# S5 rotation tables from two short power ladders, squares of x summed on VectorE, and other ranks for the input and table tasks

## The chip, the core and the metric

The kernel runs on one NeuronCore of a Trainium2 chip. Its engines are TensorE (PE in the profile; its weight loads PEld), VectorE (DVE), ScalarE (ACT) and GpSimd (POOL), and SyncE (SP) issues most DMAs. The metric is the device time of one execution in microseconds (us), as the median of several. The profile comes from one execution with the hardware profiler.

## What is computed

One decoder layer on x of 1024 x 1024 float32. Three branches share one input projection, and their gated outputs go through one output projection; a gated per-layer input embedding and a final norm follow.

```python
hn = rms_norm(h, norm_g[i])
proj = hn @ w_in[i]
rg_x, rg_gate, gq, gk, gv, gz, gb, ga, s5_u, s5_gate = split_columns(proj)
...
y_rg = rg_lru(xr, ...) * silu(rg_gate)
y_gdn = gdn_branch(gq, gk, gv, gz, gb, ga, ...)          # 8 heads, gated delta rule in chunks
y_s5 = s5_ssm(s5_u, ...)                                  # 32 groups of 16 channels, 64 complex states each
    bu = einsum('gnc,sgc->sgn', b_bar, ub)
    _, xs = associative_scan(linear_combine, (lam_bar, bu))
    y = real(einsum('gcn,sgn->sgc', c_mat, xs)) + d_g * ub
z5 = gelu(y_s5); y_s5 = z5 * sigmoid(z5 @ s5_w_glu + s5_b_glu) * silu(s5_gate)
h = h + concatenate([y_rg, y_gdn, y_s5]) @ w_out[i]
gate = sigmoid(rms_norm(h, ple_norm_g[i]) @ ple_w_gate[i])
h = h + gate * (p[i] @ ple_w_proj[i])
return rms_norm(h, final_norm_g)
```

## The kernel before, in words

Products of float32 accuracy are made of three fast ones: each operand is split into a rounded high half and the rest (`hhi`, `hlo` for the normed input; `whi`, `wlo` for a weight), and hi·hi, lo·hi and hi·lo are summed in PSUM. A projection of one block of 128 columns is 48 such matmuls of 512 columns: two halves of the sequence, eight 128-row blocks k of the input, three products each (`project`). The weight's halves are made by one ScalarE cast (`whi`) and one VectorE subtraction (`wlo`) for each block.

The program begins with the product of p and its projection (`ple_proj`, tiles `ph`, `pl`, 96 matmuls). Beside it `norm_x` prepares the input: for each half of the sequence, squares of the eight blocks of x on ScalarE (`squares`), their column sums, a reciprocal square root in some 13 tiny VectorE steps, a broadcast through TensorE (`scale`), and for each block (`split`) one VectorE product into `xt`, one ScalarE cast into `hhi` and one VectorE subtraction into `hlo`.

Then the blocks are projected in a fixed order: x0 s0 e0 g0 x1 s1 e1 g1 x2 s2 e2 g2 x3 s3 e3 g3 (x and e: RG-LRU input and gate of a tile of 128 channels; s and g: S5 input and gate), k0 k1 k2 q0 v0 z0 (DeltaNet heads 0 to 2), and then k3 q1 v1 z1, k4 and so on, with the DeltaNet work of the heads between them. k4 is asked for only when the state chain of head 0 is done.

S5 is worked in tiles of eight groups. `s5_base` computes the powers of the states once; `s5_tables` makes for each tile the matrices `s_Q`, `s_G`, `s_Kp` and the rotations `s_C`, `s_S` (cosine and sine of 1 to 128 steps of eight positions, 64 states of eight groups in two partition halves). `s5_post` uses them: product of `s_QT` with the input `s_U`, rotation by `s_C` and `s_S` (one swap of partition halves by DMA, `s_Vs`), a scan (`s_Z`), rotation back (`s_Zs`, `s_X`), and the products `s_MT`·`s_U` + `s_G`·`s_X`. `s5_out` reads the result back in another layout (`s_Yc`), adds the direct term and applies gelu.

All of this is issued by a planner in the kernel's own code: work is a list of generator tasks, sorted by a rank from the table `PRIO` (lower first). After each projection matmul, `tick` issues the steps of those tasks that its price model calls ready, and each engine's instructions are then pinned in the order of issue. So the ranks decide at build time in which order VectorE, ScalarE and TensorE meet their work, and no engine overtakes at run time. `need` and `wait` hold back further projections until given tasks are issued.

Of the kernel before, what the change touches and what calls it, by code (L numbers as in the profile page):

```python
# [22 lines left out]
P = 128  # L23
# [12 lines left out]
ORDER = [(z[0], int(z[1])) for z in "x0 s0 e0 g0 x1 s1 e1 g1 x2 s2 e2 g2 x3 s3 e3 g3".split()]  # L36
SLOTS = dict(raw=2, cy=1, kT=4, dec=2, AT=3, qT=2, AQ=2, vn=2, sz=2, XT=2, kd=1, on=1, sA=1, sW=1)
# [8 lines left out]
class Trunk:  # L46
# [9 lines left out]
    PRIO = dict(squares=2, colsum=2, scale=2, split=2, drain=-1, save=-0.5, conv=1, gates=2, blocks=2, part_g=1, s5_out=1, shift=-1, k_post=1, q_post=1, v_post=-0.5, chain=1, chain_out=-1, finish=1, solve=1, levels=1, glu_prep=0.5, pre=1, glu_post=2, split_late=1, split_soon=-0.5, add=-0.5, ple_norm=2, s5_base=0.5, s5_tables=2, decay=2, decay_late=-1, wstream=-1, mstream=0.5)  # L56
# [283 lines left out]
    def norm_x(self, hpool, sp, startup, key):  # L340
# [23 lines left out]
        def squares(half, box, sums):  # L364
            box.append(self.ps(self.psg, [P, 4, KB]))
            for k in range(KB):
                yield "a", lambda: there[half, k] <= self.now
                z = sq[k % 2][:, k // 2 % 2]
# [8 lines left out]
        def scale(half, box, sums):  # L377
            yield "v", lambda: len(sums) == KB and all(t.done for t in sums)
            ss = sp.tile([P, 4], F32, name=f"xss{half}")
            nc.vector.tensor_reduce(out=ss, in_=box[0], axis=mybir.AxisListType.X, op=ALU.add)  # L380
            z = self.rstd_of(sp, ss, 1.0 / D, EPS, 4, f"xr{half}", 1)
            while True:
                try:
                    next(z)
                except StopIteration as e:
                    r = e.value
                    break
            yield "pe", self.psg
            rb = self.ps(self.psg, [P, 512], KB)
            for t in range(4):  # L390
                self.mm(out=rb[:, t * P:(t + 1) * P], lhsT=r[:, t:t + 1].to_broadcast([P, P]), rhs=self.ident, start=True, stop=True)
            for k in range(KB):
                self.spawn(split(half, k, rb), "v")
# [11 lines left out]
        for half in range(2):  # L405
            box, sums = [], []
            self.spawn(squares(half, box, sums), "a", room=lambda half=half: there[half, 0] <= self.now and self.room(self.psg))
            self.spawn(scale(half, box, sums), "v", room=lambda sums=sums: len(sums) == KB)
# [312 lines left out]
    def s5_base(self, keep, pool):  # L721
# [10 lines left out]
        wide = pool.tile([P, 32, 28], F32, name="s_w", bufs=1)  # L732
        yield "v"
# [64 lines left out]
        for j in range(8):  # L798
            l = 7 - j
            cpy(Aq[H0, :, j], pr[H0, :, l])  # L800
            cpy(Aq[H1, :, j], pi[H1, :, l])
            ng(Bq[H0, :, j], pi[H0, :, l])
            cpy(Bq[H1, :, j], pr[H1, :, l])
            if j % 2:
                yield
# [5 lines left out]
        c8, s8 = keep.tile(sh, F32, name="s_c8"), keep.tile(sh, F32, name="s_s8")  # L811
# [11 lines left out]
        ng(s8[H1], s8[H1])  # L823
        self.s5r = (c8, s8, R8)

    def s5_tables(self, i, pool, tabs):
# [52 lines left out]
        c8, s8, R8 = self.s5r  # L879
        v.tensor_copy(out=C[:, :, 0], in_=c8[:, gs])  # L880
        v.tensor_copy(out=Sn[:, :, 0], in_=s8[:, gs])
        n = 1
        uw = t.rearrange("p g l o -> p (g l o)")
        u, w = (uw[:, 512 * z:512 * z + 512].rearrange("p (g k) -> p g k", g=8) for z in range(2))
        while n < P:
            bc = lambda a: a[:, :, n - 1:n].to_broadcast([P, 8, n])
            self.cmul(v, C[:, :, n:2 * n], Sn[:, :, n:2 * n], C[:, :, :n], Sn[:, :, :n], bc(C), bc(Sn), u[:, :, :n], w[:, :, :n])
            n *= 2
            yield
        Kp = self.slot("AT", [16, 8, P], "s_Kp")  # L890
        for q in range(2):
            pool_ = (self.psc, self.pso)[q]
            yield "pe", lambda: part.done and part.ready <= self.now and self.room(pool_)
            pt = self.ps(pool_, [16, 4, P])
            for k in range(4):
                gg = 4 * q + k
                self.mm(out=pt[:, k, 0:16], lhsT=Qf[:, gg, 112:128], rhs=G0[:, gg, :], start=True, stop=True)
                self.mm(out=pt[:, k, 16:128], lhsT=Qf[:, gg, 112:128], rhs=Gf[:, gg, 0:112], start=True, stop=True)
            yield "a"
            nc.scalar.copy(out=Kp[:, 4 * q:4 * q + 4, :], in_=pt)  # L900
        tabs.extend((QT, Kp, Gf, C, Sn, R8[:, gs]))
# [27 lines left out]
    def s5_post(self, i, uP, tabs):  # L929
# [75 lines left out]
    def s5_out(self, i, uP, box):  # L1005
# [4 lines left out]
        yield "v"  # L1010
        nc.vector.scalar_tensor_tensor(out=f(Yc), in0=f(uP), scalar=self.s5d[:, i:i + 1], in1=f(Yc), op0=ALU.mult, op1=ALU.add)
# [614 lines left out]
    def build(self):  # L1626
        tc, nc = self.tc, self.nc
        with ExitStack() as st:
# [28 lines left out]
            with ExitStack() as s5s:  # L1657
# [9 lines left out]
                self.s5d = self.load(s5k, "s5_d", [P, 4])  # L1667
# [7 lines left out]
                for kind, i in ORDER:  # L1675
                    if kind == "s":
# [47 lines left out]
def layout(x, norm_g, w_in, rg_lambda, gdn_a_log, gdn_dt_bias, **kw):  # L1724
# [39 lines left out]
def program(shapes):  # L1764
    nc = bacc.Bacc("TRN2", target_bir_lowering=False, num_devices=1)
# [13 lines left out]
```

## Time and profile before

| | |
|---|---|
| median of 3 runs | 1248.16 us (1247.47 to 1253.04) |
| profiled execution: its time, its span | 1246.3 us, 1244.6 us |
| TensorE busy | 1134.6 us (91%), mean granted clock 0.956 |
| VectorE busy | 798.5 us (64%) |
| ScalarE busy | 552.4 us (44%) |
| GpSimd busy | 158.7 us (13%) |

Busy shares are means over stages with different limits. Times in the rows below count from the span's start; L402 is line 402 of the kernel before. A wait is put down to the instruction whose end released the waiting one.

### The profile page before, as it was taken

The page shows a single profiled execution, that of the slowest core. Times are in us where ns is not written, and L with a number is a line of the kernel's source. Part 1 is how long each engine was busy: PE and PEld are TensorE (multiplying, and loading weights), DVE is VectorE, ACT ScalarE, POOL GpSimd, SP SyncE. Part 2 cuts the span into 40 slices and gives each one's busy share as a digit, 9 for nine tenths or more (in the row PEclk, how much of TensorE's full clock was granted, in tenths as well). Part 3 has the DMA queues.
Part 4 walks back from the last instruction along what each step waited for, and adds up shares of the span by engine and source line. Part 5 has one row for each costly group of instructions (what it writes and reads, how often), then busy time and mean ns, then how long its engine had stood idle before and what let it go on. Part 6 is the DMA issues. An engine that isn't in the chain of part 4 may idle for free. (4 is left out here: it accounts for less than half of the span.)

```text
span 1244.6 us, 17541 instructions
## 1 busy us (share of the span) xinstructions
PE 1134.6 (91%) x6277; PEld 926.8 (74%) x6277; DVE 798.5 (64%) x2051; ACT 552.4 (44%) x1127; POOL 158.7 (13%) x166
## 2 busy tenths in 40 slices
PE   6968899999963789999999999999978999999996
PEld 5846687787853578888888888888766778878885
DVE  3498596878773675886678767865754334254675
ACT  3433457645562646335443535344652233243432
POOL 0010000000101100000000000000063023034442
PEclk9878999999986889999999999999988899999998
DMA  7220334443654512122212221212354355364222
GB/s 241 85 85 17 87 102 123 133 143 95 206 160 139 156 51 86 31 85 52 90 30 102 52 89 31 85 35 77 128 196 148 121 187 194 116 209 152 82 71 98
DMA packets 82774, 135.98 MB, mean 109 GB/s; under 512 B 31360, under 2 KB 41792, under 8 KB 82688
## 3 DMA queue, kind: packets, MB, share of 16 engines
q1 hardware_dynamic: 81536, 130.68, 33.5%
q0 software_dynamic: 1152, 4.19, 0.9%
q8 instruction: 49, 0.80, 0.3%
q14 instruction: 37, 0.30, 0.1%
HBM read 97.98 MB, written 31.49 MB: 104 GB/s over the span
## 5 line engine op out<-in xcount | busy, mean ns | idle before, releaser
L194 PE MATMUL pp<-hhi,whi 128*128 128x512 f32 x768 | 315.2, 410 | 19.2 <-ACT hhi L399 8.3
L194 PE MATMUL pp<-hlo,whi 128*128 128x512 f32 x768 | 316.2, 412 | 3.9 <-DVE hlo L402 3.9
L194 PE MATMUL pp<-hhi,wlo 128*128 128x512 f32 x768 | 314.5, 410 | 0.0
L194 PEld LDWEIGHTS pp<-hhi,whi 128*128 128x128 f32 x768 | 146.7, 191 | 51.7 <-ACT hhi L399 11.3
L194 PEld LDWEIGHTS pp<-hlo,whi 128*128 128x128 f32 x768 | 146.7, 191 | 35.7 <-DVE hlo L402 6.2
L194 PEld LDWEIGHTS pp<-hhi,wlo 128*128 128x128 f32 x768 | 146.7, 191 | 28.7 <-issue 2.8
L472 DVE SCALAR_TENSOR_TENSOR cy<-raw,c_gdn_conv_w,cy 128x512 f32<-128x512 f32 x144 | 107.3, 746 | 11.3 <-ACT cy L468 7.3
L1471 DVE TENSOR_TENSOR mhl<-mr,mhl 128x512 fp32r<-128x512 f32 x64 | 53.2, 833 | 93.1 <-ACT mhl L1469 93.1
L194 PE MATMUL pg<-ws,mhl 128*128 128x512 f32 x384 | 102.9, 403 | 0.2 <-ACT mhl L1469 0.2
L420 DVE TENSOR_TENSOR wlo<-wraw,whi 128x1024 fp32r<-128x1024 f32 (+1 forms) x52 | 63.1, 1213 | 46.6 <-ACT whi L418 44.1
L1471 POOL TENSOR_TENSOR ws<-wsr,ws 128x512 fp32r<-128x512 f32 x48 | 66.9, 1395 | 199.8 <-ACT ws L1469 199.7
L194 PEld LDWEIGHTS pg<-ws,mhl 128*128 128x128 f32 x384 | 72.4, 191 | 19.5 <-DVE mhl L1471 1.5
L1469 ACT CAST mhl<-mr 128x512 fp32r<-128x512 f32 x64 | 39.8, 621 | 97.4 <-DMA mr<-mix 48.6
L194 PE MATMUL pp<-ws,fth 128*128 128x512 f32 x256 | 81.4, 397 | 0.0
L482 ACT COPY raw<-pp 128x512 f32<-128x512 f32 x56 | 32.6, 584 | 88.4 <-PE pp L194 85.1
L418 ACT CAST whi<-wraw 128x1024 fp32r<-128x1024 f32 (+1 forms) x52 | 52.7, 1014 | 23.6 <-DMA wraw<-in_w_blk 23.1
L194 PEld LDWEIGHTS pp<-ws,fth 128*128 128x128 f32 x256 | 48.1, 188 | 10.6
L194 PE MATMUL pp<-ws,mhl 128*128 128x512 f32 x192 | 52.5, 408 | 3.2 <-ACT mhl L1469 2.1
L194 PE MATMUL pp<-ws,ftl 128*128 128x512 f32 x128 | 51.1, 399 | 0.0
L1469 ACT CAST ws<-wsr 128x512 fp32r<-128x512 f32 x48 | 29.7, 620 | 43.9 <-DMA wsr<-in_w_out 22.9
L1293 ACT ACTIVATE osq<-on 128x128 f32<-128x128 f32 x64 | 19.6, 307 | 64.9 <-DVE on L1290 50.0
L1267 DVE TENSOR_SCALAR V<-pc,bp 128x128 f32<-128x128 f32 x64 | 22.2, 348 | 39.0 <-PE pc L194 38.5
(398 smaller groups left out, 2097.3 us busy)
## 6 DMA issues: line engine op xcount, KB each, us to landing
wraw<-in_w_blk SPq DMA_DIRECT2D x48, 512.0 KB, 3.9
mr<-mix SPq DMA_DIRECT2D x64, 256.0 KB, 3.0
dec<-dec SPq DMA_DIRECT2D x16, 512.0 KB, 5.0
wsr<-in_w_out SPq DMA_DIRECT2D x32, 256.0 KB, 2.8
xt<-in_xT SPq DMA_DIRECT2D x16, 256.0 KB, 6.0
ppd<-po POOLq DMA_DIRECT2D x8, 512.0 KB, 3.3
gcb<-grow SPq DMA_DIRECT2D x8, 512.0 KB, 5.6
dec<-gcb SPq DMA_DIRECT2D x8, 512.0 KB, 2.7
```

Of the source, the lines that this page charges most:

```text
L194: self.nc.tensor.matmul(**kw)
L418: nc.scalar.copy(out=hi, in_=raw)
L420: nc.vector.tensor_tensor(out=lo, in0=raw, in1=hi.bitcast(F32), op=ALU.subtract)
L472: nc.vector.scalar_tensor_tensor(out=y[:, sl], in0=raw[:, j + sl.start:j + sl.stop], scalar=wconv[:, j:j + 1], in1=y[:, sl], op0=ALU.mult, ...
L482: nc.scalar.copy(out=raw[:, 3 + 512 * half:3 + 512 * half + 512], in_=ps)
L1267: v.tensor_scalar(out=V, in0=p2, scalar1=bp[:, t:t + 1], scalar2=None, op0=ALU.mult)
L1293: nc.scalar.activation(out=sq, in_=on[:, t, :], func=AF.Square, accum_out=d["so"][:, t:t + 1])
L1469: nc.scalar.copy(out=hl[:, 0, :], in_=raw)
L1471: e.tensor_tensor(out=hl[:, 1, :], in0=raw, in1=hl[:, 0, :].bitcast(F32), op=ALU.subtract)
```

## The change

The squares of a half are summed by seven VectorE additions (`total`), so four one-column matmuls remain for each half instead of 32. The rotations come from two ladders of powers built once in `s5_base` (`s_cb`, `s_sb`: 1 to 16 steps; `s_ca`, `s_sa`: 0 to 7 times 16 steps), packed so that all 128 partitions hold different states; a table is then six products of 128 x 512, eight DMAs that spread it over both partition halves, and a negation on ScalarE, where there were seven doubling levels of six products. The powers are used in rising order, so 32 small copies become four, and the positions in `s_U` and `s_MT` are reversed to fit. The direct term moves from `s5_out` into the diagonal of `s_Kp`. The ranks of the input tasks and of `s5_tables` are lowered, the pool for `s_Yc` is opened at s1 or earlier, and the scratch space for POOL's DMAs is set to 8192.

```diff
-    PRIO = dict(squares=2, colsum=2, scale=2, split=2, ..., s5_base=0.5, s5_tables=2, ...)
+    PRIO = dict(squares=-0.9, total=-0.9, scale=-0.9, split=-0.9, ..., s5_base=0.5, s5_tables=-0.3, ...)
...
+                z = sq[1][:, half] if k == 0 else sq[0][:, len(tots) % 2]
                 nc.scalar.activation(out=z, in_=xt[k][:, H[half]], func=AF.Square)
-                sums.append(self.spawn(colsum(z, box[0], k), "pe", sums[-1:]))
-
-        def colsum(z, ss, k):
+                if k:
+                    tots.append(self.spawn(total(z, sq[1][:, half]), "v", tots[-1:]))
+                    sums.append(tots[-1])
+
+        def total(z, acc):
+            nc.vector.tensor_tensor(out=acc, in0=acc, in1=z, op=ALU.add)
+            yield
...
             for t in range(4):
-                self.mm(out=ss[:, t, k:k + 1], lhsT=z[:, t * P:(t + 1) * P], rhs=self.ones[:, 0:1], start=True, stop=True)
+                self.mm(out=ss[:, t:t + 1], lhsT=sq[1][:, half, t * P:(t + 1) * P], rhs=self.ones[:, 0:1], start=True, stop=True)
...
+        for n in (1, 2, 4, 8):
+            bc = lambda a: a[:, :, n - 1:n].to_broadcast([P, 16, n])
+            self.cmul(v, cb[:, :, n:2 * n], sb[:, :, n:2 * n], cb[:, :, :n], sb[:, :, :n], bc(cb), bc(sb), u[:, :, :n], w[:, :, :n])
+            yield
...
+        for n, e in ((1, 1), (2, 2), (4, 3)):
...
-        while n < P:
-            bc = lambda a: a[:, :, n - 1:n].to_broadcast([P, 8, n])
-            self.cmul(v, C[:, :, n:2 * n], Sn[:, :, n:2 * n], C[:, :, :n], Sn[:, :, :n], bc(C), bc(Sn), u[:, :, :n], w[:, :, :n])
-            n *= 2
-            yield
+        for o, p, q, r_, u, op in ((C4, ca, cb, sa, sb, ALU.subtract), (S4, sa, cb, ca, sb, ALU.add)):
+            v.tensor_tensor(out=o, in0=xa(p), in1=xb(q), op=m)
+            yield
+            v.tensor_tensor(out=W4, in0=xa(r_), in1=xb(u), op=m)
+            yield
+            v.tensor_tensor(out=o, in0=o, in1=W4, op=op)
+            yield
+        yield "d"
...
+                for ho in (H0, H1):
+                    nc.sync.dma_start(out=flat(dst[ho, g4, :]), in_=src[hs])
+        yield "a"
+        nc.scalar.mul(out=Sn[H1], in_=Sn[H1], mul=-1.0)
...
+        v.tensor_tensor(out=Kp[:, :, 0:16], in0=Kp[:, :, 0:16], in1=self.dd[:, gs, :], op=ALU.add)
...
-        nc.vector.scalar_tensor_tensor(out=f(Yc), in0=f(uP), scalar=self.s5d[:, i:i + 1], in1=f(Yc), op0=ALU.mult, op1=ALU.add)
...
+                    if not box and (i == 1 and kind == OPEN or g.done and base.done):
+                        self.need(g, base)
+                        sbs.close()
+                        box.append(s5s.enter_context(tc.tile_pool(name="s5y", bufs=1)))
...
-    nc = bacc.Bacc("TRN2", target_bir_lowering=False, num_devices=1)
+    nc = bacc.Bacc("TRN2", target_bir_lowering=False, num_devices=1, dynamic_dma_scratch_size=8192)
```

Since the ranks sort the tasks, the order of instructions moves on every engine. Three places follow; the number at the end of a name is the buffer's.

On VectorE, where the second half of x is split, before: `xt` is the norm's product, `hlo` the low half, and `s_Q`, `s_G`, `s_tmp`, `s_tmg`, `s_w` belong to the first S5 table.

```order
L397 SCALAR_TENSOR_TENSOR xt<-xt,c_norm_g,pg 128x512
L847 TENSOR_TENSOR s_Q<-s_w,s_Aq 128x1024
L402 TENSOR_TENSOR hlo<-xt,hhi 128x512
L847 TENSOR_TENSOR s_G<-s_w,s_Ag 128x1024
L849 TENSOR_TENSOR s_tmp<-s_w,s_Bq 128x1024
L849 TENSOR_TENSOR s_tmg<-s_w,s_Bg 128x1024
L851 TENSOR_TENSOR s_Q<-s_Q,s_tmp 128x1024
L851 TENSOR_TENSOR s_G<-s_G,s_tmg 128x1024
L847 TENSOR_TENSOR s_w<-s_w,s_Ag 128x128
```

And of the change, the same place, from the last step of `s5_base`'s first part on.

```order
L785 TENSOR_TENSOR s_ki_559<-s_small_114 128x32
L402 SCALAR_TENSOR_TENSOR xt_137<-xt_137,c_norm_g_153,pg_568 128x512
L402 SCALAR_TENSOR_TENSOR xt_138<-xt_138,c_norm_g_153,pg_568 128x512
L402 SCALAR_TENSOR_TENSOR xt_139<-xt_139,c_norm_g_153,pg_568 128x512
L407 TENSOR_TENSOR hlo_119<-xt_137,hhi_118 128x512
L407 TENSOR_TENSOR hlo_119<-xt_138,hhi_118 128x512
L407 TENSOR_TENSOR hlo_119<-xt_139,hhi_118 128x512
L402 SCALAR_TENSOR_TENSOR xt_140<-xt_140,c_norm_g_153,pg_568 128x512
```

The splits stood between, and behind, the steps of `s5_base` and of the first table; now all sixteen stand together ahead of the ladders and the tables, which follow beside the first projections.

On TensorE, where the last S5 tile meets the projections, before: the last matmul of k2, and behind it the tile's products (`s_U`, `s_QT`, `s_MT`, `s_X`, `s_G`) among those of the DeltaNet keys (`kT`).

```order
L194 MATMUL pp_2829<-hhi_116,wlo_2699 128x512
L194 MATMUL pg_2905<-s_U_2846,s_QT_2275 128x128 x4
L194 MATMUL pg_2925<-kT_2641 128x128 x4
L194 MATMUL pg_2937<-s_U_2846,s_QT_2275 128x128 x4
L194 MATMUL pg_2926<-kT_2641 128x128 x4
L194 MATMUL pg_3033<-s_U_2846,s_MT_2855 128x128
L194 MATMUL pg_3033<-s_X_3024,s_G_2235 128x128
```

And of the change: the last products of the same tile, inside projection k2; its `s_QT` products stand some 100 rows earlier, inside k0.

```order
L195 MATMUL pp_2667<-hhi_118,wlo_2616 128x512
L195 MATMUL pg_2688<-kT_2451 128x128 x4
L195 MATMUL pp_2667<-hhi_118,whi_2615 128x512
L195 MATMUL pp_2667<-hlo_119,whi_2615 128x512
L195 MATMUL pp_2667<-hhi_118,wlo_2616 128x512
L195 MATMUL pg_2701<-s_U_2415,s_MT_2424 128x128
L195 MATMUL pg_2701<-s_X_2669,s_G_2016 128x128
```

Before, nothing of a projection stands between the first and the last product of the tile; now about 100 projection matmuls do, and 34 of k2 and all of q0 follow.

On TensorE, in the state chain of DeltaNet head 0, before: each chunk of the chain has a product from `R`, two from `V` and two from `Sm`, here with matmuls of v1 and z1 (`pp`) between.

```order
L197 MATMUL pg_3991<-ident_64,kT_2491 128x128
L194 MATMUL pp_3898<-hlo_117,whi_3557 128x512
L194 MATMUL pg_3998<-qT_3548,kT_2641 128x128 x4
L194 MATMUL pp_3898<-hhi_116,wlo_3558 128x512
L194 MATMUL pc_4012<-R_4003,XT_3589 128x128
L194 MATMUL pp_4017<-hhi_116,whi_3689 128x512
L194 MATMUL pp_4017<-hlo_117,whi_3689 128x512
L194 MATMUL pp_4017<-hhi_116,wlo_3690 128x512
```

And of the change, behind the last matmul of z1.

```order
L195 MATMUL pc_3931<-R_3914,XT_3583 128x128
L195 MATMUL pc_3940<-V_3936,kd_3918 128x128
L195 MATMUL po_3902<-V_3936,AQ_3228 128x128
L195 MATMUL pc_3952<-Sm_3945,kT_2451 128x128
L195 MATMUL po_3954<-Sm_3945,qT_2879 128x128
L198 MATMUL pg_3956<-ident_64,kT_2451 128x128
L195 MATMUL pc_3966<-R_3960,XT_3583 128x128
```

The chain's steps of chunks 2 to 7 now follow each other without projection matmuls up to k4: of its steps from `R`, `V` or `Sm` 17 stand directly behind another one there, where before it was 2.

## Rows read from the trace of the kernel before

**Rows 1.** Waits of TensorE: releaser, us in total, times, longest us.

```profile
PE pg L194 <- DVE s_X L989: 13.6, 1, 13.6
...
PE pg L194 <- DVE AT L1093: 9.2, 1, 9.2
PE pp L194 <- ACT hhi L399: 8.3, 5, 2.2
```

**Rows 2.** Busy us of each engine by stretch, granted clock, DMA share, GB/s.

```profile
12.50:69.20 56.70, 56.70 (x250) 48.68 (x250) 24.83 (x77) 27.06 (x51) 5.38 (x8) 0.94 0.39 141
69.20:107.30 38.10, 22.62 (x72) 13.33 (x71) 35.84 (x115) 8.04 (x14) 2.66 (x4) 0.69 0.17 51
107.30:340.00 232.70, 229.05 (x1135) 183.66 (x1134) 179.73 (x365) 126.18 (x171) 6.79 (x13) 0.99 0.42 121
340.00:460.00 120.00, 75.14 (x362) 61.72 (x361) 72.52 (x215) 61.77 (x115) 12.85 (x17) 0.83 0.43 127
460.00:526.10 66.10, 64.56 (x531) 53.74 (x531) 46.49 (x142) 32.41 (x82) 2.63 (x6) 1.00 0.22 62
```

**Rows 3.** Timeline of TensorE in the first stage: start us, us, engine, line, instruction.

```profile
19.57 1.70 PE L194 MATMUL pg<-ones,xsq 128*128 128x1 f32 x8
...
37.07 0.63 PE L194 MATMUL pg<-ph,pl 128*128 128x512 f32 x1
...
60.06 0.39 PE L194 MATMUL pp<-ph 128*128 128x512 f32 x1
...
105.92 0.40 PE L194 MATMUL pp<-hhi,whi 128*128 128x512 f32 x1
```

**Rows 4.** Timeline of VectorE in the first stage.

```profile
5.32 0.18 DVE L691 TENSOR_SCALAR s_small<-c_s_log_dt 128x32 f32<-128x32 f32 x1 [5.32 <-DMA c_s_log_dt<-in_s_log_dt]
...
34.96 0.19 DVE L380 TENSOR_REDUCE xss<-pg 128x4 f32<-128x32 f32 x1 [5.45 <-PE pg L194]
...
48.75 2.06 DVE L397 SCALAR_TENSOR_TENSOR xt<-xt,c_norm_g,pg 128x512 f32<-128x512 f32 x3 [9.66 <-PE pg L194]
...
103.64 0.69 DVE L402 TENSOR_TENSOR hlo<-xt,hhi 128x512 fp32r<-128x512 f32 x1 [0.16 <-ACT hhi L399]
```

**Rows 5.** Groups of VectorE: count, busy us, mean ns, idle before and releaser.

```profile
L397 DVE SCALAR_TENSOR_TENSOR xt<-xt,c_norm_g,pg 128x512 f32<-128x512 f32 x16 | 11.4, 744 | 9.7 <-PE pg L194 9.7
L402 DVE TENSOR_TENSOR hlo<-xt,hhi 128x512 fp32r<-128x512 f32 x16 | 10.5, 687 | 0.2 <-ACT hhi L399 0.2
L714 DVE TENSOR_TENSOR s_tmp<-s_S 128x8 f32<-128x8 f32 (+6 forms) x28 | 9.5, 340 | 0.4
...
L716 DVE TENSOR_TENSOR s_C<-s_C 128x8 f32<-128x8 f32 (+6 forms) x28 | 8.5, 305 | 0.0
L1011 DVE SCALAR_TENSOR_TENSOR s_Yc<-s_uP,c_s_d,s_Yc 128x1024 f32<-128x1024 f32 x4 | 5.1, 1283 | 11.2 <-DMA s_Yc<-yd 11.2
```

**Rows 6.** Groups by shape: the one-column matmuls of TensorE, the large table products of VectorE.

```profile
L194 PE MATMUL pg<-ones,xsq 128*128 128x1 f32 x128 | 22.5, 299 | 10.9 <-ACT xsq L369 10.9
L851 DVE TENSOR_TENSOR s_Q<-s_Q,s_tmp 128x1024 f32<-128x1024 f32 x4 | 4.9, 1224 | 0.1
```

**Rows 7.** Timeline of TensorE, 391 to 526 us.

```profile
391.38 0.77 PE L194 MATMUL pg<-s_X,s_G 128*128 128x128 f32 x2 [13.62 <-DVE s_X L989]
...
523.45 0.49 PE L194 MATMUL pc<-Sm,kT 128*128 128x128 f32 x2 [0.38 <-DVE Sm L1279]
...
525.59 0.46 PE L194 MATMUL po<-V,AQ 128*128 128x128 f32 x2 [0.59 <-DVE V L1267]
525.80 0.48 PE L194 MATMUL pp<-hhi,whi 128*128 128x512 f32 x1
```

**Rows 8.** Timeline of ScalarE around a table load.

```profile
339.73 1.28 ACT L1038 ACT_TABLE_LOAD   x1
341.02 0.63 ACT L1038 ACTIVATE kT<-cy 128x512 f32<-128x512 f32 x1
```

**Rows 9.** DMA issues: queue, count, KB each, median us to landing.

```profile
s_Vs<-s_V SPq DMA_DIRECT2D x8, 256.0 KB, 3.7
```

More of the change, by code (lines that the diff above doesn't have):

```diff
@@ L55 @@
     AHEAD = (0, 0.3, 0.3, 0)
-    PRIO = dict(squares=2, colsum=2, scale=2, split=2, drain=-1, save=-0.5, conv=1, gates=2, blocks=2, part_g=1, s5_out=1, shift=-1, k_post=1, q_post=1, v_post=-0.5, chain=1, chain_out=-1, finish=1, solve=1, levels=1, glu_prep=0.5, pre=1, glu_post=2, split_late=1, split_soon=-0.5, add=-0.5, ple_norm=2, s5_base=0.5, s5_tables=2, decay=2, decay_late=-1, wstream=-1, mstream=0.5)
+    PRIO = dict(squares=-0.9, total=-0.9, scale=-0.9, split=-0.9, drain=-1, save=-0.5, conv=1, gates=2, blocks=2, part_g=1, s5_out=1, shift=-1, k_post=1, q_post=1, v_post=-0.5, chain=1, chain_out=-1, finish=1, solve=1, levels=1, glu_prep=0.5, pre=1, glu_post=2, split_late=1, split_soon=-0.5, add=-0.5, ple_norm=2, s5_base=0.5, s5_tables=-0.3, decay=2, decay_late=-1, wstream=-1, mstream=0.5)
     def __init__(self, tc, ins, out):
@@ L362, in norm_x, with squares, scale @@
         sq = [self.slot(tag, [P, 2, 512], "xsq") for tag in ("cy", "kd")]
[L364 to L365 removed]
+        tots = []
+        def squares(half, sums):
             for k in range(KB):
[L367 to L368 removed]
+                yield "a", lambda: there[half, k] <= self.now and all(t.done for t in tots[:-1])
+                z = sq[1][:, half] if k == 0 else sq[0][:, len(tots) % 2]
                 nc.scalar.activation(out=z, in_=xt[k][:, H[half]], func=AF.Square)
[L370 to L380 removed]
+                if k:
[4 more added lines that the diff above has]
+            yield
+        def scale(half, sums):
+            yield "pe", lambda: len(sums) == KB - 1 and all(t.done and t.ready <= self.now for t in sums) and self.room(self.psg)
+            ss = self.ps(self.psg, [P, 4])
+            for t in range(4):
+                self.mm(out=ss[:, t:t + 1], lhsT=sq[1][:, half, t * P:(t + 1) * P], rhs=self.ones[:, 0:1], start=True, stop=True)
+            yield "v"
             z = self.rstd_of(sp, ss, 1.0 / D, EPS, 4, f"xr{half}", 1)
@@ L405, in norm_x @@
         for half in range(2):
-            box, sums = [], []
-            self.spawn(squares(half, box, sums), "a", room=lambda half=half: there[half, 0] <= self.now and self.room(self.psg))
-            self.spawn(scale(half, box, sums), "v", room=lambda sums=sums: len(sums) == KB)
+            sums = []
+            self.spawn(squares(half, sums), "a", room=lambda half=half: there[half, 0] <= self.now)
+            self.spawn(scale(half, sums), "pe", room=lambda sums=sums: len(sums) == KB - 1)
     def weight(self, key):
@@ L732, in s5_base @@
         wide = pool.tile([P, 32, 28], F32, name="s_w", bufs=1)
+        self.s5d = self.load(pool, "s5_d", [16, 32])
         yield "v"
@@ L797, in s5_base @@
         cpy = lambda o, i_: v.tensor_copy(out=o, in_=i_)
[L798 to L805, printed above, removed]
+        cpy(Aq[H0], pr[H0, :, 0:8])
+        cpy(Aq[H1], pi[H1, :, 0:8])
+        ng(Bq[H0], pi[H0, :, 0:8])
+        cpy(Bq[H1], pr[H1, :, 0:8])
+        yield
         cpy(Ag[H0], pr[H0])
@@ L810, in s5_base @@
         self.s5p = (Aq, Bq, Ag, Bg)
-        c8, s8 = keep.tile(sh, F32, name="s_c8"), keep.tile(sh, F32, name="s_s8")
+        c8, s8 = T("s_c8"), T("s_s8")
         R8 = keep.tile(sh, F32, name="s_R8")
@@ L939, in s5_post @@
         for j in range(8):
-            nc.sync.dma_start(out=U[16 * j:16 * j + 16], in_=src[j])
+            nc.sync.dma_start(out=U[16 * j:16 * j + 16], in_=src[7 - j])
         MT = self.slot("XT", [P, 8, P], "s_MT")
```

60 lines of the change are left out of this document (40 added, 20 removed).

## The prediction

> **What bounds the kernel now.** I read the table of engines first. TensorE is busy 91% of the span, so the time can only fall where TensorE stands idle or runs slowly, or where its work is taken away. The list of what it waited for comes next [rows 1]: its longest single wait is 13.6 us for one VectorE result of S5 (`s_X`), and five waits for the cast `hhi` of the input sum to 8.3 us. The windows then say where that falls [rows 2]. From 107.3 to 340 us TensorE is busy 229.05 of 232.7 us and from 460 to 526.1 us 64.56 of 66.1; there is next to nothing to win. Two stretches are loose. From 69.2 to 107.3 us TensorE works 22.62 of 38.1 us at a granted clock of 0.69, while VectorE works 35.84: that is projection x0, waiting for the second half of the input, whose last `hlo` comes at 103.64 [rows 4]. From 340 to 460 us TensorE stands idle 44.9 of 120 us at a clock of 0.83, and VectorE is busy only 72.52 us: no engine is full there, so it is a chain, that of the last S5 tile (the 13.6 us end at 391.38 [rows 7]), with the DeltaNet solve of heads 0 and 1 behind it, while k2 has been projected and nothing else may go.
>
> The stretch from 12.5 to 69.2 us is full, but badly: it holds the 128 one-column matmuls, 22.5 us of TensorE [rows 6], and beside them a 512-column matmul shows 0.63 us where later it shows 0.39 [rows 3].
>
> **Part 1: start to the end of x0.** Before, the first matmul of s0 stands at 105.92 [rows 3]. Of the 128 one-column matmuls 112 go, 19.7 us by the row. Then TensorE no longer bounds this part; VectorE does, and its order up to the last `hlo` is listed in the change: 81 tiny steps at 0.19 us [rows 4], 15.4; 16 norm products, 11.9, and 16 low halves, 10.5 [rows 5]; 14 additions of squares and 8 `pl`, all 128x512 float32 operations of two tensors like `hlo`, at 0.69 us, 15.2; two `wlo` of 128x1024 at 1.22 us [rows 6], 2.4. The sum is 55.4 us. It starts at 5.3 us, so the last `hlo` comes no earlier than 60.7, and x0's last matmuls some 2 us later: 63. That assumes that VectorE has no wait which its other steps don't fill; before, it waited 5.45 and 9.66 us for the sums and the broadcast of one half [rows 4], so the upper bound is about 75. The lower one is 58, where tiny steps overlap. I take 63, because the 5.45 and the 9.66 us both ended on TensorE, whose queue is now empty of the column sums. What stood between the splits (most of `s5_base` and the first table) moves behind them. Term 1: 105.9 - 63 = 43 us earlier.
>
> **Part 2: s0 to k4.** Before, it takes from 105.9 to 525.8 us [rows 7], 419.9 us, with TensorE busy 229.05 + 75.14 + 64.56 = 368.8 [rows 2]. I rebuild it from work and waits.
> Work: the gate matmuls and the transposes of `s_Q`, which stood beside x0, now fall behind it, +3.3 us (an estimate, 16 small ones at some 0.2 us). The work at a clock of 0.83 runs nearer full, and of 75.14 us about 10 go. That leaves 362.
> Waits, first those that go: the last tile's products now stand inside projections k0 to k2 with about 100 projection matmuls between the first and the last of them (the second pair of pieces of the order). The wait of 13.6 us is then covered, and so is most of the 44.9.
> What stays or comes: the 3.65 and 1.54 us of the two full stretches, 5.2; at s1 the order holds projections until gates and base are issued, 3; between q0 and z0 5; and the new one. k4 waits for head 0's state chain, and of its steps 17 now follow each other with no projection matmul between, against 2 before (the third pair). A step takes 1.07 us, half of the way from 523.45 to 525.59, and the two products in it some 0.46 [rows 7], so 15 more bare steps leave 15 x 0.61 = 9 us idle, and with solve steps of heads 2 and 3 beside them on VectorE 12. A lower clock in those 12 us and around: 3. VectorE meets a table's work (six 128x1024 products at 1.22, six of 128x512 at 0.69, some dozen small ones: 14 us) within one projection of TensorE's about 10 us more than once between s1 and g1; the low halves `wlo` of the next weights queue behind it: 4. Together 32.
> So 362 + 32 = 394, against 419.9: term 2 is 26 us. k4 starts at 63 + 394 = 457 where it was 525.8.
>
> **Part 3: k4 to the end.** The order of projections, solves and chains is the same there. No term: 0, within 5 us either way.
>
> **What lies off the path.** On VectorE the six lines of the doubling (28 instructions each, the first 9.5 and the last 8.5, 53.4 us together) and the direct term (5.1) go [rows 5]; 24 products of 128x512 at 0.69 (16.6), ladders of 42 tiny operations at 0.19 to 0.34 (10) and the additions of squares (9.7) come: -22 us of 798.5. This is worth something only where VectorE leads, and those places are in terms 1 and 2. The 32 new DMAs (eight for each table, 128 KB) have `s_Vs` as their nearest row, 256 KB in 3.7 us [rows 9]. The reader of a table stands a projection or more behind it, so I take 0; if that cover failed, each table would cost an issue of eight and a landing, some 7 us, 28 in all. On SyncE's queue the table's eight stand behind their products and ahead of later weights; these are asked for several projections early, so I take 0, bounded by the same 28. ScalarE's negation is hidden. The seven extra table loads that the order shows on ScalarE (45 before, 52 after) cost 1.28 us each [rows 8], 9.0 us; ScalarE is busy 126.18 of 232.7 us in the full stretch, so I take 0 and keep 9. The smaller scratch for POOL's DMAs has no row here; POOL works 13% of the span, I take 0, bounds -5 to +5 by the 6.79 us that POOL did in the full stretch.
>
> On a load of a table the row and a page differ: the next activation starts at 341.02, 1.29 us after the load began, and no drain is seen [rows 8]. The Trainium skill's "ScalarE: Activation LUTs", section "What ACT_TABLE_LOAD costs", puts a drain of about 1.38 us beside the load, 2.66 us together. By the page seven more would be 18.6 us where the row says 9.0; no run here shows the drain.
>
> **The sum.** 1246.3 - 43 - 26 = 1177.3, so 1177 us. It is made against the profiled execution, 1246.3 us; the median of the runs shown is 1248.16, 1.9 above it, and I leave that in the range.
>
> On the new bare steps a page speaks against the change: at 340 to 460 us a stretch with gaps was granted 0.83 and one without 0.99 [rows 2]. The Trainium skill's "TensorE: Matmul & The Clock Gate", section "HAM oscillation — how this bites in real kernels", says that idle gaps between bursts send the clock down, and that the next burst pays for it. By that rule the 17 bare steps would be worked at the lower level and their products take twice as long: 17 x 0.46 = 8 us, where I put 3; the sum would be 1182. The rows agree with its direction.
>
> **The rivals.**
> *Only the start is won.* The idle time from 340 to 460 us may belong to the DeltaNet solve and its slots, not to S5: the 9.2 us wait for `AT` [rows 1] is the solve's. Against it, the longest single wait is that for `s_X`, and the solve's products stand behind the tile's in the order. Then the time is 1246.3 - 43 + 3 = 1206.
> *The second half comes late all the same.* VectorE's steps are in program order, and a late sum or a late piece of x stops all behind it; x0 would end at about 85, halfway. For it: the waits of rows 4. Time 1177 + 22 = 1199.
> *Table loads decide,* if all seven stand on the path: 1177 + 9 = 1186. By the page named above it would be 1196.
> *Slower: VectorE becomes the bound from s0 to k4.* The tables now rank ahead of the weights' low halves, so each projection may stand behind table work. Price: four tables of 14 us and some 120 small operations of base and ladders at about 0.25, 30: 86 us, which beside x0 had been paid already in idle time of TensorE. If all of it is bare, 1177 + 86 = 1263. It decides from 71 us on, above 82% of it. Against it: VectorE is busy 179.73 of 232.7 us in the full stretch and held TensorE up for only 3.65 [rows 2].
> *The change moves nothing,* because both stretches only shift their idle time to k4: 1248.
>
> **How the numbers follow.** Forecast 0.65; only the start 0.17; late second half 0.08; table loads 0.04; VectorE the bound 0.04; nothing moves 0.02. The likeliest case has its own range: 1156 if the new waits (32) are a third of what I put, to 1190 if x0 ends at 75. The range goes on to 1207, which takes in the first three rivals and leaves out about 2 in 10 with the tails of the forecast. Differences under 0.5% are no change by this measurement: faster 0.94, same 0.02, slower 0.04.
>
> **What would show it.** The first matmul of s0 at about 63 us (58 to 75) and sixteen one-column matmuls. No wait of over 3 us for `s_X`. K4's first matmul at 457, with waits for `R`, `V` and `Sm` of some 10 us ahead of it. VectorE busy about 776 us. From k4 to the end the same 718 us. Wrong would be: waits on `wlo` or `whi` between s1 and g3 of over 15 us (VectorE the bound), or idle time of some 40 us still standing between k2 and k4 (the solve was the chain).

## The result: 1207.7 us, and the profile after

The median went from 1247.82 to 1207.66 us (four runs, 1201.29 to 1212.08); the ratio is 0.9675, with a 95% interval of 0.9613 to 0.9738. Faster was right; the predicted 1177 us was not, and the range ended at 1207. The profiled execution took 1201.29 us (span 1199.6), 45 us less than that of before.

The start of a projection is the first of its 16 `hhi`·`whi` matmuls on the timeline of TensorE:

| start, us | s0 | e1 | k0 | q0 | k4 | end of span |
|---|---|---|---|---|---|---|
| before | 105.9 | 177.5 | 315.4 | 400.7 | 525.8 | 1244.6 |
| changed | 65.5 | 153.5 | 308.1 | 356.8 | 486.6 | 1199.6 |
| predicted | 63 | | | | 457 | 1176 |

So 40 us were won by s0, as forecast; of these only 7 were left at k0; by q0 it was 44, and at k4 39. First the windows between these points, before (columns as in [rows 2]; the first number behind the length is TensorE's busy time):

```profile
105.90:315.40 209.50, 205.85 (x1007) 163.80 (x1006) 164.53 (x335) 113.21 (x140) 2.52 (x8) 0.99 0.38 109
315.40:400.70 85.30, 54.02 (x304) 46.11 (x303) 52.03 (x145) 44.65 (x87) 10.29 (x11) 0.84 0.54 159
400.70:525.80 125.10, 109.97 (x724) 89.77 (x723) 83.24 (x243) 63.68 (x141) 9.46 (x17) 0.95 0.30 88
525.80:1244.60 718.80, 685.27 (x3929) 564.34 (x3928) 433.99 (x1121) 290.88 (x688) 127.28 (x110) 0.98 0.32 105
```

And of the changed kernel, cut at the same projections:

```profile
65.50:308.10 242.60, 221.98 (x1087) 175.83 (x1086) 166.13 (x310) 121.47 (x151) 4.41 (x11) 0.95 0.43 117
308.10:356.80 48.70, 43.20 (x218) 36.98 (x216) 34.07 (x72) 31.03 (x55) 4.07 (x6) 0.93 0.65 199
356.80:486.50 129.70, 116.59 (x747) 94.35 (x747) 91.41 (x289) 84.14 (x177) 14.40 (x20) 0.94 0.36 108
486.50:1199.60 713.10, 682.44 (x3929) 561.30 (x3928) 434.44 (x1122) 291.32 (x688) 128.49 (x110) 0.98 0.33 106
```

The reader is to see that s0 to k0 became 33 us longer: 16 us more busy (80 more matmuls, of gates and of the third and fourth S5 tile) and 17 more idle. k0 to q0 became 37 us shorter: 26 of it idle time that went, 11 work that now stands ahead of k0. From s0 to k4 the idle time fell from 50 to 39 us only, and the busy time rose from 370 to 382.

The waits of TensorE in the changed kernel (releaser, us in total, times, longest), against [rows 1]:

```profile
PE pg L195 <- DMA s_MT<-s_Kp: 9.8, 1, 9.8
...
PE pg L195 <- DVE s_X L1028: 6.5, 2, 5.2
PE pc L195 <- DVE Sm L1316: 5.5, 6, 2.7
PE pc L195 <- DVE R L1292: 4.8, 1, 4.8
PE pc L195 <- DVE V L1304: 4.7, 9, 0.8
...
PE pp L195 <- ACT hhi L404: 2.3, 3, 1.5
```

`s_X` fell from 13.6 to 6.5 and `hhi` from 8.3 to 2.3. New is the first row (9.2 us for `ph`, not shown, are the beginning of the program). Its name is that of the DMA that ended last; the waiting instruction reads `s_U`. Its place on TensorE's timeline, with the last matmul of s1 ahead of it, and then the chain ahead of k4:

```profile
138.21 0.40 PE L195 MATMUL pp<-hhi,wlo 128*128 128x512 f32 x1
148.40 2.05 PE L195 MATMUL pg<-s_U,s_QT 128*128 128x128 f32 x8 [9.79 <-DMA s_MT<-s_Kp]
...
153.51 0.69 PE L195 MATMUL pp<-hhi,whi 128*128 128x512 f32 x1
...
468.88 0.49 PE L195 MATMUL pc<-Sm,kT 128*128 128x128 f32 x2 [0.52 <-DVE Sm L1316]
...
475.97 0.80 PE L195 MATMUL pc<-Sm,kT 128*128 128x128 f32 x2 [1.59 <-DVE Sm L1316]
...
486.14 0.76 PE L195 MATMUL po<-V,AQ 128*128 128x128 f32 x2 [0.54 <-DVE V L1304]
486.55 0.77 PE L195 MATMUL pp<-hhi,whi 128*128 128x512 f32 x1
```

On SyncE's queue, why `s_U` comes so late:

```profile
137.31 0.33 SPq L860 DMA_DIRECT2D s_w<-in_s_b_re  x1
...
139.51 0.33 SPq L974 DMA_DIRECT2D ud<-s_uP  x1
142.44 3.65 SPq L979 DMA_DIRECT2D s_U<-ud  x8
146.20 5.19 SPq L986 DMA_DIRECT2D s_MT<-s_Kp  x8
```

`s_uP` of s0 lies ready from 78.7 us, but the write stands behind the end of table 0, whose first large product VectorE reaches at 108.21:

```profile
108.21 1.22 DVE L873 TENSOR_TENSOR s_Q<-s_w,s_Aq 128x1024 f32<-128x1024 f32 x1
...
138.63 0.27 DVE L939 TENSOR_TENSOR s_Kp<-s_Kp,s_dd 16x128 f32<-16x128 f32 x1
```

Before, that product stood at 94.6 us, beside x0, and the write of `s_uP` at 135.7. So s0 came 40 us earlier, table 0 began 14 us later, and the write, with the shorter table ahead of it, came 4 us later.

The sizes of the steps came out: the last `hlo` of the input ended at 64.7 us, and in the groups, against [rows 5, 6]:

```profile
L195 PE MATMUL pg<-ones,xsq 128*128 128x1 f32 x16 | 2.0, 244 | 1.4 <-DVE xsq L377 1.4
L402 DVE SCALAR_TENSOR_TENSOR xt<-xt,c_norm_g,pg 128x512 f32<-128x512 f32 x16 | 11.1, 742 | 1.8 <-PE pg L195 1.8
L407 DVE TENSOR_TENSOR hlo<-xt,hhi 128x512 fp32r<-128x512 f32 x16 | 10.2, 684 | 0.0
L377 DVE TENSOR_TENSOR xsq<-xsq 128x512 f32<-128x512 f32 x14 | 9.6, 686 | 2.5 <-ACT xsq L371 2.5
L917 DVE TENSOR_TENSOR s_tmp<-s_tmp,s_C 128x512 f32<-128x512 f32 x8 | 5.5, 688 | 0.1
s_C<-s_tmp SPq DMA_DIRECT2D x16, 128.0 KB, 2.4
```

VectorE is busy 776.5 us (776 was said). 52 table loads stand on ScalarE.

### The profile page after: what moved, and what is told of

It reads as the page before. It is cut to its first block, busy times and chain, and to the rows that moved or that the text cites. A ratio compares the mean times of both kernels' runs of the same rounds, so it can differ in the third digit from the quotient of the medians.

```text
span 1199.6 us, 17257 instructions
## 1 busy us (share of the span) xinstructions
PE 1111.2 (93%) x6165; PEld 902.7 (75%) x6165; DVE 776.5 (65%) x1933; ACT 566.2 (47%) x1138; POOL 159.6 (13%) x166
## 5 line engine op out<-in xcount | busy, mean ns | idle before, releaser
L1330 ACT ACTIVATE osq<-on 128x128 f32<-128x128 f32 x64 | 19.7, 308 | 75.8 <-DVE on L1327 57.9
```

Source lines behind the costliest of these rows:

```text
L1330: nc.scalar.activation(out=sq, in_=on[:, t, :], func=AF.Square, accum_out=d["so"][:, t:t + 1])
```

## The experiments

Each is measured against the kernel before on the same chip, where the median of that was 1243.8 to 1247.8 us; so differences of a few us between rows go by the ratios, whose intervals are 95%. The starts are those of one profiled execution each. That of the changed kernel was the fastest of its four, 6 us below its median.

| run | time, us | ratio, interval | s0 | q0 | k4 |
|---|---|---|---|---|---|
| changed kernel | 1207.7 | 0.9675, 0.9613 to 0.9738 | 65.5 | 356.8 | 486.6 |
| e1 input ranks only | 1237.5 | 0.9941, 0.9918 to 0.9963 | 106.4 | 397.5 | 519.5 |
| e2 sums on TensorE | 1224.7 | 0.9833, 0.9785 to 0.9881 | 107.0 | 375.2 | 503.8 |
| e3 old input ranks | 1204.6 | 0.9654, 0.9601 to 0.9707 | 87.6 | 350.1 | 487.5 |
| e4 early `s_U` | 1207.5 | 0.9694, 0.9655 to 0.9734 | 65.2 | 352.8 | 490.6 |
| e5 ladders only | 1232.1 | 0.9894, 0.9856 to 0.9932 | 102.1 | 392.1 | 512.4 |
| e6 start only | 1225.1 | 0.9837, 0.9807 to 0.9868 | 65.5 | 379.0 | 508.7 |
| e7 short solve | 1193.1 | 0.9584, 0.9549 to 0.9619 | 67.4 | 358.4 | 474.8 |
| e8 solve ranks | 1193.7 | 0.9584, 0.9551 to 0.9617 | 66.7 | 359.5 | 486.9 |
| e9 base, gates earlier | 1183.4 | 0.9501, 0.9471 to 0.9531 | 69.6 | 353.0 | 471.4 |
| e10 base first | 1194.4 | 0.9589, 0.9556 to 0.9621 | 86.0 | 353.2 | 480.1 |
| e11 solve on GpSimd | 1201.0 | 0.9647, 0.9618 to 0.9676 | 67.5 | 361.2 | 495.6 |
| e12 base only | 1197.2 | 0.9624, 0.9603 to 0.9645 | 67.7 | 354.5 | 482.1 |
| e13 gates only | 1216.5 | 0.9790, 0.9767 to 0.9812 | 67.3 | 367.4 | 495.2 |
| e14 e8 and e9 | 1187.9 | 0.9552, 0.9533 to 0.9572 | 69.6 | 351.0 | 480.1 |

**What wins the start?** The ranks alone, on the kernel before:

```diff
-    PRIO = dict(squares=2, colsum=2, scale=2, split=2, ...
+    PRIO = dict(squares=-0.9, colsum=-0.9, scale=-0.9, split=-0.9, ...
```

> The kernel before with one edit: the ranks of squares, column sums, scale and split are -0.9 (they were 2); column sums stay on TensorE, tables stay as they were. If the start is won by the order of VectorE's steps, s0 comes at about 80 us (TensorE's product of p and 128 one-column matmuls fill it to 69 us as before, and x0's 48 matmuls follow without waiting), 26 us of the 40 that the whole change won there, and the time is 1220 to 1230. If it is won by taking the column sums off TensorE, s0 stays above 95 us and the time above 1237.

The second held: s0 did not move. The splits were done (their last `hlo` at 69 to 71 us instead of 104), but `pl` now stood behind them on VectorE, and with it the product of p on TensorE:

```profile
69.55 0.80 PE L194 MATMUL pg<-pl,ph 128*128 128x512 f32 x1 [10.02 <-DVE pl L1419]
```

x0 then ran without a break from 95.5 to 106.4. The other way round, on the changed kernel, `total` is replaced by the old `colsum`:

```diff
-                    tots.append(self.spawn(total(z, sq[1][:, half]), "v", tots[-1:]))
+                sums.append(self.spawn(colsum(z, box[0], k), "pe", sums[-1:]))
```

> The changed kernel with one part undone: the squares go to TensorE's 128 one-column matmuls again, at rank -0.9. If the additions on VectorE are worth what the 112 removed matmuls took (19.7 us by their row), s0 comes at 80 to 85 us instead of 65.5 and the time is 1215 to 1225. If the order alone wins the start, s0 stays below 70 us and the time is within 6 us of the changed kernel's 1207.

The time fell into the first window; the place didn't, s0 came at 107.0. The additions on VectorE are worth 17 us at these ranks, and more at s0 than at the end. The changed kernel with the old ranks:

```diff
-    PRIO = dict(squares=-0.9, total=-0.9, scale=-0.9, split=-0.9, ...
+    PRIO = dict(squares=2, total=2, scale=2, split=2, ...
```

> The changed kernel with the ranks of squares, sums, scale and split back at 2. If the ranks win the start, s0 is back above 90 us; the wait for s_U between s1 and e1 (9.8 us in the changed kernel) is then gone, since table 0 has those 25 us more, so the time is only 15 to 25 us above the changed kernel's, 1222 to 1232. If the ranks don't matter beside the additions on VectorE, s0 stays below 75 us and the time is within 6 us.

Half a miss for both: s0 came 22 us later, and the time was the same. Here table 0 came first (its first large product at 83.2 us), and the S5 tiles stood no later than in the changed kernel. So 22 of the 40 us at s0 are worth nothing at the end. At q0 this kernel is even 7 us ahead of the changed one, since TensorE hardly waits from s0 to q0; it loses them again in the chain ahead of k4, at a lower clock:

```profile
87.60:350.10 262.50, 254.62 (x1293) 204.60 (x1292) 179.92 (x285) 153.69 (x205) 7.54 (x16) 0.99 0.52 147
350.10:487.50 137.40, 128.03 (x748) 105.89 (x747) 92.16 (x291) 78.33 (x173) 13.48 (x20) 0.83 0.31 96
```

**Is the wait for `s_U` a cost by itself?** The write and the loads are spawned behind the projection, not inside `s5_post`:

```diff
+        u = self.spawn(early(), "d", tables[1:] + self.drains[-1:], prio=-0.9)
+        t = self.spawn(self.s5_post(i, ub, tabs), "d", tables + [u])
```

> The changed kernel with one edit: the write of s_uP to memory and the eight loads of s_U are issued as soon as the projection is drained and the tile before is done with s_U, not when the table is done. If the wait of 9.8 us between s1 and e1 is a cost by itself, it goes and all behind it comes 8 to 12 us earlier: k4 at 475 to 479 us, the time 1196 to 1200. If k4 hangs on the DeltaNet path (decay, key products, solve, levels, chain) whatever the projections do, k4 stays within 4 us of 486.6 and the time within 4 us of 1207.

The second held. The wait went and three others took its place (waits of TensorE, 65 to 357 us):

```profile
PE pp L195 <- DVE wlo L425: 7.3, 2, 7.0
PE pc L198 <- DVE s_Q L877: 6.0, 1, 6.0
PE pg L195 <- DVE s_X L1035: 3.8, 2, 3.0
```

All three are VectorE's: e1 came 5.8 us earlier, k0 0.9 later. So the DMA by itself costs nothing at the end: without it TensorE waits for other results of VectorE. That table 0's late place on VectorE is the cause is not shown by this; the order of base, gates and table 0 is tried below.

**Are there two gains that add up?** First the S5 part alone, then the rest alone:

```diff
-    PRIO = dict(squares=-0.9, total=-0.9, ..., s5_tables=-0.3, ...
+    PRIO = dict(squares=2, colsum=2, ..., s5_tables=2, ...
```

> The kernel before with the S5 part of the change alone (two ladders, packed tables, powers in rising order, direct term in s_Kp, s_Yc opened earlier, scratch of 8192); column sums on TensorE and all ranks as before. Theory of the S5 path (k4 comes when four S5 tiles, then the DeltaNet solve and chain have run one after the other): s0 stays at about 106 us, the tiles follow each other every 54 to 58 us instead of 72, k4 comes at 495 to 505 and the time is 1212 to 1222, most of the gain without any of the start. Theory of the terms (40 us won at the start, nothing behind): the time is 1238 to 1248.

> The kernel before with the other part alone: squares summed on VectorE, input tasks at rank -0.9 and tables at -0.3; the seven doubling levels stay. Theory of the S5 path: s0 comes at about 65 us as in the changed kernel, the tiles follow each other every 68 to 74 us, k4 comes at 512 to 528 and the time is 1232 to 1248, so the 40 us are lost before k4. Theory of the terms: k4 at 486 or 26 us behind that, the time 1207 to 1215.

Neither theory held; both lie between. Ladders alone won 13 us and the start alone 20; the whole change won 40, with an interval of 33 to 48, so the times alone hardly tell whether the two add up or help each other. The smaller parts (direct term, `s_Yc`, scratch) were in no run alone. In the start alone s0 stood at 65.5, yet the 40 us halved by k4. Its waits, 65 to 330 us:

```profile
PE pp L194 <- DVE wlo L424: 13.4, 2, 11.7
PE pc L194 <- DVE gg L563: 13.3, 1, 13.3
PE pc L194 <- ACT egl L584: 3.6, 1, 3.6
```

This is the rival of the prediction in which VectorE becomes the bound: with the doubling levels still in the tables, `wlo` and the gates (`gg`) queue behind them, 27 us. The ladders remove that work: in the changed kernel `wlo` costs 1.3 us from s0 to k4 and `gg` nothing.

**The chain ahead of k4.** 8 of the 31 steps of the first solve; the other 23 are left out:

```diff
-        for j in range(31):
+        for j in range(31 if h0 else 8):
```

> The changed kernel with 8 of the 31 column steps of the first solve (heads 0 and 1); the rest of that solve is left out, so the output is not the reference's. Theory of the path: VectorE's 62 us between the load of its matrix and the store fall to some 16, levels and chain run beside q1 and v1, k4 comes 20 to 25 us earlier (as far as TensorE's idle time and the bare chain reach) and the time is 1182 to 1190. If the solve lies beside projections that bound the time anyway, k4 moves by less than 6 us and the time stays above 1200.

Between the two: k4 came 11.7 us earlier, and q0 to k4 took 116.4 us instead of 129.7, at a clock of 0.99 instead of 0.94:

```profile
358.40:474.80 116.40, 110.25 (x748) 90.32 (x747) 74.58 (x243) 83.23 (x176) 14.10 (x20) 0.99 0.40 120
```

Of the 13 us that went, 7 were idle time and 6 work at a lower clock. The bare chain is behind both, as far as a run shows it that also takes 17 us of work off VectorE. The prediction had put 12 + 3.

```diff
-    ... k_post=1, ... chain=1, ... solve=1, levels=1, ...
+    ... k_post=-0.4, ... chain=-0.4, ... solve=-0.4, levels=-0.4, ...
```

> The changed kernel with k_post, solve, levels and chain at rank -0.4 (they were 1), so that their steps stand ahead of the convolution's on VectorE. Theory of the path: the solve takes 45 to 55 us instead of 62, k4 comes 8 to 15 us earlier, the time is 1190 to 1200. If the planner already issues each step as soon as its operands are there, the order moves little and the time stays within 5 us of 1207.

The time came, its reason didn't: the solve still took 61 us and k4 stood at 486.9; what the traces show of the gain lies behind k4 (705 us to the end instead of 713). And the first solve on GpSimd, with those ranks:

```diff
-        e, lane = (nc.gpsimd, "g") if h0 >= SOLVE_G else (nc.vector, "v")
+        e, lane = (nc.gpsimd, "g") if h0 == 0 else (nc.vector, "v")
```

> The kernel with the raised solve ranks, and the first solve (heads 0 and 1) on GpSimd, which is busy 13% of the span, in place of VectorE. If the solve is late because its 62 small steps share VectorE with convolutions and weights, it takes 45 us or less from the load to the store instead of 61, k4 comes at 470 to 478 instead of 486.9 and the time is 1180 to 1188. If GpSimd's steps are no faster than VectorE's with all it shares, the solve takes 58 us or more and the time is 1192 to 1200.

The second held: 65.6 us from the load to the store, and k4 9 us later; the time was 1 us above its window.

**The order of base, gates and table 0.** On the changed kernel:

```diff
-    ... gates=2, ... s5_base=0.5, ...
+    ... gates=0, ... s5_base=-0.5, ...
```

> The changed kernel with s5_base at rank -0.5 (it was 0.5) and gates at 0 (it was 2). If the wait of 9.8 us between s1 and e1 is table 0 being late on VectorE, behind base and gates, the table's first large product comes before 100 us (108.2 in the changed kernel), the write of s_uP before 132 (139.5), the wait falls below 3 us, k4 comes 6 to 10 us earlier and the time is 1196 to 1202. If other waits take its place, as when only the loads of s_U came earlier (time 1207.5), k4 and the time stay within 5 us.

Better than either: 24 us less than the changed kernel by the medians, 16 between the two profiled executions. Not for the reason given, since table 0 came only 4 us earlier (103.76). SyncE's and TensorE's timelines:

```profile
133.25 0.44 SPq L974 DMA_DIRECT2D ud<-s_uP  x1
...
136.52 3.92 SPq L979 DMA_DIRECT2D s_U<-ud  x8
```

```profile
144.46 1.05 PE L195 MATMUL pg<-s_U,s_QT 128*128 128x128 f32 x8
```

From the write to the product it is 11.2 us (8.9 in the changed kernel), but the order now has e1's matmuls ahead of the product, so nobody waits. The gates' last steps stand at 85 us (`gg`; 110 in the changed kernel). By windows:

```profile
69.60:302.90 233.30, 218.20 (x1074) 171.62 (x1073) 165.08 (x292) 117.25 (x146) 4.40 (x11) 0.96 0.44 121
302.90:353.00 50.10, 43.99 (x226) 37.45 (x224) 32.29 (x83) 33.96 (x63) 5.33 (x7) 0.94 0.71 210
353.00:471.40 118.40, 110.65 (x739) 89.69 (x739) 91.98 (x279) 76.50 (x165) 12.63 (x19) 0.99 0.37 116
471.40:1183.70 712.30, 683.41 (x3929) 563.84 (x3928) 433.42 (x1119) 290.03 (x688) 128.41 (x110) 0.97 0.32 106
```

e1 is 18 us earlier, but k0 only 5 and q0 4; the larger part, 11 us, is won from q0 to k4, at a clock of 0.99. That this is because the chain now lies beside z1 for longer (10 bare steps by the order instead of 17) is not shown: e14, whose chain has about as few, took 129.1 us there at 0.94, with a wait of 6.3 for `raw` (ScalarE). Base ahead of even the splits:

```diff
-    ... gates=2, ... s5_base=0.5, ...
+    ... gates=-0.2, ... s5_base=-0.95, ...
```

> The changed kernel with s5_base at rank -0.95, ahead of the input's splits, and gates at -0.2. s0 comes 4 to 8 us later than 65.5. If the four S5 tiles set when q0 may start, q0 comes 15 us or more ahead of 356.8, k4 as well, and the time is 1185 to 1197. If TensorE's own work is what fills s0 to q0 (265 of 291 us busy in the changed kernel), q0 comes at most 10 us earlier, and the time is 1198 to 1210.

s0 came 20 us later, more than either theory said, and q0 at 353.2, 4 us earlier: that is the second theory, although the time, 13 us below the changed kernel's by the medians, is the first's. The first write of `s_uP` stands at 121.8, 18 us ahead of the changed kernel's, and TensorE is idle for 9 us only from s0 to q0, where the changed kernel has 26:

```profile
86.00:353.10 267.10, 257.75 (x1298) 208.20 (x1297) 181.65 (x294) 158.56 (x209) 7.47 (x16) 0.98 0.50 142
```

So in e3 and here the row of S5 tiles doesn't set q0 alone; TensorE's own work fills the stretch. Then each of the two ranks of e9 alone, and both with those of the solve (the last):

```diff
-    ... gates=2, ... s5_base=0.5, ... k_post=1, ... chain=1, ... solve=1, levels=1, ...
+    ... gates=2, ... s5_base=-0.5, ... k_post=1, ... chain=1, ... solve=1, levels=1, ...
+    ... gates=0, ... s5_base=0.5, ... k_post=1, ... chain=1, ... solve=1, levels=1, ...
+    ... gates=0, ... s5_base=-0.5, ... k_post=-0.4, ... chain=-0.4, ... solve=-0.4, levels=-0.4, ...
```

> The changed kernel with s5_base alone at rank -0.5; gates stay at 2, behind the tables. If the two together won 24 us because table 0 came earlier, this wins most of it: the wait for s_U falls below 3 us, k4 comes at 472 to 478, the time is 1184 to 1192. If it was the gates (their small VectorE steps stand ahead of the tables, and all that waits for them, s1 and the decays, comes earlier), the time stays at 1198 to 1210.

> The changed kernel with gates alone at rank 0; s5_base stays at 0.5. If the gates carry the 24 us, the time is 1184 to 1192, although table 0 comes no earlier than 108 us (first large product); its products are asked for later by the order (first at g1 and not s1), so the wait for s_U goes all the same. If table 0's time carries them, the time stays at 1198 to 1210.

> The changed kernel with both sets of ranks that won something: s5_base -0.5 and gates 0, and k_post, solve, levels and chain -0.4. If their gains lie in different places (before k4 by 15 us, behind k4 by 7), they add up to 1170 to 1178. If both remove the same bare steps ahead of k4, the time is that of the first alone, 1180 to 1187.

Base alone won 10 us (its interval overlaps the changed kernel's), gates alone lost 9, both won 24; the solve's ranks added nothing to them. None of the three fell into a window that was forecast: e12 and e14 came 1 us beside their second, e13 6 us above both. The ranks do not act one by one: each shifts where the planner puts the others' work (that this is the reason is argued from the orders). In e13 the product of `s_U` again stands where TensorE waits for it (16.5 us in two waits). e9 is the best kernel found; its interval lies below that of the changed kernel.

## Why the prediction was wrong

**Right.** s0 at 65.5 (63 said, 58 to 75), sixteen column sums, VectorE's sum of small steps, and that the idle time between k0 and q0 goes (from 31 to 5.5 us). No wait of TensorE names the tables' own DMAs or ScalarE's negation. Nearly right: from k4 on 5.7 us were won where 0 was said, within 5; the wait for `s_X` fell from 13.6 to 6.5 us, but its longest is 5.2 where no wait over 3 was to be left. The size of the bare chain came out (about 13 us, 15 put), but not its parts: less idle time (12 put, 7 measured) and more work at a low clock (3 put, 6 measured).

**Wrong: term 2.** s0 to k4 was to take 394 us, 362 of work and 32 of waits and clock; it took 421.0, with TensorE busy 381.8 and idle 39.2, where before it took 419.9. So 20 of the 27 us that are missing lie in the work and 7 in the waits.

*"The work at a clock of 0.83 runs nearer full, and of 75.14 us about 10 go. That leaves 362."* The credit was never there. The projections' matmuls alone, before (s0 to k4, and the window of that clock) and after (s0 to k4):

```profile
105.90:525.80 419.90, 306.87 (x1201) 224.35 (x1200) 0.00 (x0) 29.89 (x51) 0.95 0.39 113
340.00:460.00 120.00, 56.41 (x218) 42.16 (x217) 0.00 (x0) 5.11 (x9) 0.83 0.43 127
```

```profile
65.50:486.50 421.00, 304.89 (x1201) 225.99 (x1200) 0.00 (x0) 30.00 (x51) 0.95 0.43 123
```

2 us went, not 10. In the window of 0.83 a projection matmul took 0.259 us, where the mean from s0 to k4 is 0.255: there was 1 us to win. The low clock stood mostly over idle time, as from 370 to 394 us:

```profile
370.00:394.00 24.00, 3.39 (x14) 3.16 (x15) 12.58 (x31) 3.72 (x12) 3.64 (x3) 0.51 0.42 117
```

The other work rose. The gates' matmuls and the transposes of `s_Q` took 5 us more (3.3 was put). The new waits brought low clock of their own: the `s_U`·`s_QT` products took 2 us more (2.05 us for the eight behind the wait, where the first eight before took 1.05), and the five products of the chain 19.7 us instead of 14.3. The last piece of the chain ran at a granted clock of 0.50, and the same pair of products that took 0.49 us takes 0.80 (timeline above):

```profile
475.90:487.10 11.20, 9.50 (x31) 7.24 (x32) 9.29 (x35) 3.76 (x12) 0.00 (x0) 0.50 0.00 0
```

That is the rule which the prediction weighed from the Trainium skill, "TensorE: Matmul & The Clock Gate", section "HAM oscillation — how this bites in real kernels": idle gaps lower the clock and the next work pays. The trace agrees that the work behind pays (0.80 where 0.49); the gaps need not be long here, as the last section shows.

*"At s1 the order holds projections until gates and base are issued, 3."* From s1 to e1 TensorE did not wait 3 but 2.9 ahead of s1 and 9.8 behind it, and its idle time in s0 to k4 was 39 us where the waits other than clock were 29. The waiting product is the first of `s5_post` that uses table 0, and of such a reader the prediction said *"The reader of a table stands a projection or more behind it, so I take 0"*. What the first part moved behind the splits, base, gates and table 0, was counted by its work on TensorE (3.3) and not by the time at which VectorE gets to it. That its place matters is shown by e9 (15 us earlier at k4 by ranks of base and gates alone; 4 of them by q0, 11 from there) and e3 (s0 22 us later, table 0 25 us earlier, q0 7 us earlier). But no run shows that the 9.8 us are lost at the end: in e4 they went and others came. How much each of base, gates and table 0 carries is not settled, since e12 and e13 do not add up to e9.

**The rivals.** "Only the start is won" gave the right number, 1206, by the wrong way: the idle time at 340 to 400 did go, and what was lost was the start's gain, between s0 and k0. With the ladders in and s0 anywhere from 65 to 88, q0 came at 350 to 361 us in ten of eleven kernels (the other is gates alone, 367). One thing that fits is the row of four S5 tiles, each some 54 us behind the one before in the changed kernel (writes of `s_uP` at 139.5, 195.5, 249.2 and 300.8), 72 us before (135.7 to 351.1). It is not the only bound, since in e3 and e10 the row came earlier and q0 hardly did, with TensorE busy nearly throughout: there a later s0 leaves TensorE full, and in the changed kernel an earlier one leaves it waiting, mostly for what VectorE has still to do. VectorE as the bound showed in the start alone (27 us of waits); in the whole change it did not show as waits for `wlo` (1.3 us), but its queue is what `s_U` waited behind. For the table loads no run was made; TensorE's waits for ScalarE from s0 to k4 sum to 7.7 us, where before it was 20.6.

## What to carry to other kernels

When work is moved out of the way of a start, follow it to its first reader: its new time decides, not its size. Two parts of a change that share an engine need not add up, as base and gates here, so each wants a run alone, and the sum of terms a check against what the other part hides. The mean clock of a window need not be the clock over its work; take the pitch of a known matmul inside it.

## What had not been expected of the hardware

In the changed kernel the granted clock fell to 0.50, the lower of its two levels, between 474 and 475 us, inside the one gap of 1.59 us in a chain of 128x128 products whose other gaps were 0.2 to 0.6 us. It stayed there to about 492, 5 us into the next projection. The long gap is not what it takes: in e8 (raised ranks of the solve) the same chain lost the clock at about 471 us with gaps of 0.54, 0.52 and 0.54 just ahead, and in e12 at about 465.

```profile
469.93 0.49 PE L195 MATMUL pc<-R,XT 128*128 128x128 f32 x2
470.95 0.62 PE L195 MATMUL pc<-V,kd 128*128 128x128 f32 x2 [0.54 <-DVE V L1304]
...
473.26 0.79 PE L195 MATMUL pc<-R,XT 128*128 128x128 f32 x2
```
